# Branch projections of a hybrid encoder layer: operand loads in one written SyncE order, two k-pairs ahead, and the states' block sums formed inside the gate pairs

## The chip, the cores and the metric

The kernel runs on one core of one Trainium2 chip. The metric is the device time of one execution in microseconds (us); the median of several runs counts. TensorE is called PE here, VectorE DVE, ScalarE ACT, SyncE SP.

## The reference, cut to what matters

One encoder layer over 1024 tokens and 16 meta tokens, D_MODEL = 1024, all in float32. The part around the change is the middle of the layer:

```python
proj = h @ w_in                                  # split into q, k, v, z, ..., sc_b, sc_c, sc_x, gate_a, gate_b
o_dn = gated_deltanet_bidir(q, k, v, z, ...)     # its last step: o * silu(z)
y_a = o_dn @ w_branch_dn
y_b = (sc_b * depthwise_conv_centred(sc_c * sc_x, sc_conv_w)) @ w_branch_sc
merged = sigmoid(gate_a) * y_a + sigmoid(gate_b) * y_b
h_res = h_res + merged @ w_out
...
```

Before it lie the input projection with the DeltaNet scans, behind it the output projection, the SwiGLU and a final norm.

## The kernel before

**Arithmetic.** Every float32 operand is split into a high part (a cast on ACT, `split`, L101) and a low part (a subtraction on DVE, L102), and every product is three matmuls: high by high, high by low, low by high. The large products are done as 2 x 2 block products with seven block products instead of eight. Their operands are the blocks A11, A12, A22, B11, B21, B22 themselves and sums of blocks, S1 to S4 on one side and T1 to T4 on the other.

**Gate pairs.** The last thing that the input projection computes is the merge gates. A pair (`pair_steps`, L1574) takes two weight units of gates A and B, forms their block sums in place, does seven block products of 12 matmuls (named P1, P2, S2, S1, S3, S4, TT in the list `PAIR`, L1648) and puts the results into two tiles, o1 and o2, which are stored to `ta_d` and `tb_d` (L1622, L1623). Five pairs are done: pairs 0 and 1 in a hand-written order, pairs 2 and 3 by a loop (L1725), and the last one by `last_pair` (L1651). The result tiles come from the tag `s4` (L69), of which there are **four buffers**.

**States' sums.** `state_sums(k)` (L1700), four times, loads two rows of `p_d` (the short convolution's states) into two `s4` tiles, does four DVE subtractions of 512 columns and stores the result to `ts_d`. Before the change two of them are written behind each of pairs 2 and 3.

**Branch projections.** `blocks_of` (L1789) runs twice: first branch B (weights `w_bsc`, states from `p_d` and `ts_d`), then branch A (weights `w_bdn`, states `o_blocks`, which lie in SBUF). Each run goes over seven block products n = 0 to 6, each with two halves kk of the contraction. Here a half is called a k-pair and numbered q = 14*branch + 2*n + kk, so q = 0 to 27. A k-pair is 24 matmuls into four PSUM banks; products of even n go to one set of four banks, those of odd n to the other. Its operands are loaded by `loaded` (L1763, the DMA on L1767) into raw tiles, of which there are four buffers in rotation (branch B uses two a k-pair, branch A one), and split into a ring that holds the parts of four k-pairs.

After products 1, 4, 5 and 6 a quarter of the result is gated (`give`, L1801; DVE, L1805): for that, `gate_tiles` (L1793) has loaded four gate pieces into two `s4` tiles. In branch A the gated piece is also added to the other branch's (L1465).

`gated(h)` (L1715), eight times, loads a head's scan output into a big tile and its z into an `s4` tile, and multiplies them (L1723). When all eight are there, the A branch's own block sums (in `between_b(3)`) are formed on DVE: four subtractions of 128x2048 elements. `between_a` loads the eight rows of `w_out` into `s4` tiles (L1866) and splits them into the big tiles b0 to b3: four rows after product 5 of branch A, four after product 6.

Behind the projections come `merged` and `project` (L1887, L1895), whose matmuls are on L1899 to L1901.

**Order.** All these loads and stores are given out by SP. An SP instruction that waits for a buffer holds up all that stands behind it on SP. Where no manual schedule is open, the framework orders each engine's instructions by a simulation of its own, with the written order as priority; inside a manual schedule, the named engines keep the written order. Before the change nothing from pair 2 to the end of `blocks_of` is under a manual schedule.

Of the kernel before, what the change touches and what calls it, by code (L numbers as in the profile page):

```python
# [8 lines left out]
F32 = mybir.dt.float32  # L9
# [3 lines left out]
ALU = mybir.AluOpType  # L13
# [35 lines left out]
def encoder_layer(ctx: ExitStack, tc: tile.TileContext, x, meta, norm1_w, w_in, w_ba,  # L49
# [56 lines left out]
    def rawtile(shape):  # L106
        raw_slots.append(raw_slots.pop(0))
        pool, tag = raw_slots[-1]
        return pool.tile(shape, F32, tag=tag, name=uid("raw"), bufs=1)
# [1587 lines left out]
    for k in SECTION.split():  # L1697
        steps[k]()
    border0.close()
    def state_sums(k):  # L1700

        r = [s4(D) for _ in range(2)]
        for i in range(2):
            nc.sync.dma_start(r[i], p_d[4 * i + k])
        (b12, b11), (b22, b21) = ((t[:, lo], t[:, hi]) for t in r)
        sub(b11, b12, b11)
        sub(b12, b22, b12)
        sub(b22, b22, b11)
        sub(b21, b21, b22)
        for i in range(2):  # L1710
            nc.sync.dma_start(ts_d[k][:, i], r[i])
# [12 lines left out]

    for n, j in enumerate(range(GH + 2, KT - 1), 2):  # L1725
        d = pair_steps(n, j)[0]
        for k in PAIR.split():
            d[k]()
        for k in range(2):
            state_sums(2 * n - 4 + k)  # L1730
    o1 = last_pair(KT - 1 - GH, KT - 1)

    warm2 = keep.tile([P, 1], F32, name="warm2")
# [26 lines left out]
        split(h_, l_, src)  # L1760
        return h_, l_

    def loaded(f, kk):  # L1763

        raw = rawtile([P, 2, 512])
        for i in range(2):
            nc.sync.dma_start(raw[:, i], f(2 * kk + i))  # L1767
        return part(raw)

    def weight_blocks(w, sums_):  # L1770
        a = {"A11": (0, lo), "A12": (4, lo), "A22": (4, hi)}
        d = {n: lambda kk, r=r, c=c: loaded(lambda k: w[(r + k) * P:(r + k + 1) * P, c], kk) for n, (r, c) in a.items()}
        for n, i, c in (("S2", 0, lo), ("S3", 0, hi), ("S4", 1, lo), ("S1", 1, hi)):
            d[n] = lambda kk, i=i, c=c: loaded(lambda k: sums_[k][:, i, c], kk)
        return d

    state_blocks = {n: lambda kk, r=r, c=c: loaded(lambda k: p_d[r + k][:, c], kk)
                    for n, (r, c) in {"B11": (0, hi), "B21": (4, hi), "B22": (4, lo)}.items()}
    for n, i, c in (("T3", 0, lo), ("T1", 0, hi), ("T2", 1, lo), ("T4", 1, hi)):
        state_blocks[n] = lambda kk, i=i, c=c: loaded(lambda k: ts_d[k][:, i, c], kk)  # L1780

    bank_x, bank_y = [pss(), pss(), psd(), psm()], [psd(), psm(), pss(), psd()]
    pv, us = [], []

# [1 line left out]
        w = big("w2", [P, 2, 512], F32)  # L1786
        pv.extend([w[:, 0], w[:, 1], *(tp.tile([P, 512], F32, tag="t2", name=uid("t2"), bufs=2) for _ in range(2))])

    def blocks_of(a_, b_, gate_d, first, between):  # L1789

        gates = {}

        def gate_tiles(n, r, c):  # L1793
            g = [s4().rearrange("p (k c) -> p k c", k=2) for _ in range(2)]
            gates[n] = [g[t // 2][:, t % 2] for t in range(4)]
            for t in range(4):
                nc.sync.dma_start(gates[n][t], gate_d[r + t][:, c])

        where = {1: (0, hi), 4: (4, lo), 5: (0, lo), 6: (4, hi)}

        def give(n, t, y):  # L1801
            r, c = where[n]
            m_ = mg[r // 4][:, t, c]
            g = gates[n][t]
            nc.vector.scalar_tensor_tensor(out=m_ if first else g, in0=g, scalar=1.0, in1=y, op0=ALU.add, op1=ALU.mult)  # L1805
            if not first:
                add(m_, m_, g)
        for n, (a, b) in enumerate((("A11", "B11"), ("A12", "B21"), ("S2", "T2"), ("S1", "T1"), ("S3", "T3"), ("S4", "B22"), ("A22", "T4"))):
            bank = (bank_x, bank_y)[n % 2]
            fresh = n in (0, 1, 3)  # L1810
            if n in where:
                gate_tiles(n, *where[n])
            for kk in range(2):
                (ah, al), (bh, bl) = a_[a](kk), b_[b](kk)
                for t in range(4):
                    c = slice(t * P, t * P + P)
                    for k in range(2):
                        begin, end = kk + k == 0, kk + k == 2
                        mm(bank[t], ah[:, k, c], bh[:, k], start=begin and fresh, stop=False, skip_group_check=not fresh)
                        mm(bank[t], ah[:, k, c], bl[:, k], start=False, stop=False, skip_group_check=not fresh)  # L1820
                        mm(bank[t], al[:, k, c], bh[:, k], start=False, stop=end, skip_group_check=not fresh)
            if n == 0 and not pv:
                take_temps()
            if n == 2 and not us:
                w = [wp.tile([P, 2, 512], F32, tag=g, name=uid("us"), bufs=2) for g in ("wh", "wl")]
                us.extend(w[t // 2][:, t % 2] for t in range(4))
            for t in range(4):
                y = bank[t]
                if n in (0, 3):
                    nc.scalar.copy(pv[t], y)  # L1830
                elif n == 2:
                    nc.scalar.copy(us[t], y)
                elif n in (1, 4):
                    add(pv[t], y, pv[t])
                elif n == 5:
                    add(us[t], y, us[t])
            for t in range(4):
                if n in where:
                    give(n, t, (us if n == 5 else bank if n == 6 else pv)[t])
            between(n)  # L1840

    o_blocks = {}

    def between_b(n):
        if n < 2:
            for h in range(2):
                gated(4 + 2 * n + h)
        elif n == 3:
            t23 = big("b1", [P, 2, 4, 512], F32)
            t4 = big("b0", [P, 4, 512], F32)  # L1850
            b12, b11, b22, b21 = (og[i][:, :, c] for i in range(2) for c in (lo, hi))
            sub(t23[:, 1], b22, b12)
            sub(b12, b12, b11)
            sub(t23[:, 0], b22, b12)
            sub(t4, b21, t23[:, 0])
            for name, x in (("B11", b11), ("B21", b21), ("B22", b22), ("T1", b12), ("T2", t23[:, 0]), ("T3", t23[:, 1]), ("T4", t4)):
                o_blocks[name] = lambda kk, x=x: part(x[:, 2 * kk:2 * kk + 2])

    def between_a(n):
        nonlocal woh, wol  # L1860
        if n == 5:
            woh, wol = four("w")
        if n >= 5:
            for j in range(4 * (n - 5), 4 * (n - 5) + 4):
                raw = s4(D)
                nc.sync.dma_start(raw, w_out[j * P:j * P + P, :])  # L1866
                split(woh[j], wol[j], raw)

    woh = wol = None
    for h in range(4):  # L1870
        gated(h)
    blocks_of(weight_blocks(w_bsc, ss_d), state_blocks, tb_d, True, between_b)
    blocks_of(weight_blocks(w_bdn, sd_d), o_blocks, ta_d, False, between_a)

    wrow = big("w2", [P, D], F32)
    nc.sync.dma_start(wrow, norm2_w[0:1, :].broadcast_to([P, D]))
# [443 lines left out]
```

## Time and profile before

| | us |
|---|---|
| median of 3 runs | 1972.05 |
| the three runs | 1972.13, 1969.25, 1972.05 |
| the profiled execution | 1970.95 |
| its span (first to last instruction) | 1969.2 |
| PE busy in the span | 1939.6 (98%) |
| DVE busy | 1478.0 (75%) |
| ACT busy | 876.6 (45%) |
| mean granted PE clock (1 is full) | 0.995 |

Times in all rows are microseconds from the span's start. A row of a timeline has the start, the duration, the engine, the line, the operation, the tile written and the tiles read, how many instructions were merged into the row, and in brackets how long the engine sat idle before it and who ended that. SPq is SP's sequencer: its rows are the moments at which DMAs are given out, not their transfers. In a table of stretches each engine's cell is its busy time and its count of instructions; then come the granted PE clock, the mean busy share of the 16 DMA engines and the GB/s that they moved.

### The profile page before, as it was taken

The numbers are of one execution on the slowest core, as the hardware profiler recorded it, in microseconds if no ns is written. First come the engines' busy times: TensorE is split into PE (matmuls) and PEld (weight loads), VectorE is DVE, ScalarE is ACT, GpSimd is POOL, SyncE is SP. The second block draws the span as 40 slices with busy tenths as digits, with TensorE's granted clock in tenths as the row PEclk, the third lists the DMA queues.
The fourth block names the chain that finished last, engine by engine and source line by source line (L and its number), as shares of the span: only waits on it lengthen the run. The fifth ranks groups of instructions, "written<-read, shape, count | busy, mean of one in ns | idle before, by whom it ended". The sixth has DMA issues, their size and how long they took to land.

```text
span 1969.2 us, 32146 instructions
## 1 busy us (share of the span) xinstructions
PE 1939.6 (98%) x11896; PEld 1703.5 (87%) x11896; DVE 1478.0 (75%) x3117; ACT 876.6 (45%) x2016; POOL 109.4 (6%) x410
## 2 busy tenths in 40 slices
PE   9999999999999999999998899999999999999998
PEld 8999999999999999888886788888888888888887
DVE  7888688888888888867964777669676765746575
ACT  6472364646464646343443444335333333325344
POOL 2011101010101010100000000000000000000000
PEclk9999999999999999999999899999999999999999
DMA  4122122222221213375259863423366654577654
GB/s 145 59 89 79 57 87 60 76 60 76 60 78 58 85 51 108 108 260 206 86 205 346 288 197 120 147 102 115 110 230 245 246 189 153 179 277 239 194 175 166
DMA packets 141410, 286.15 MB, mean 145 GB/s; under 512 B 46844, under 2 KB 48309, under 8 KB 137797
## 3 DMA queue, kind: packets, MB, share of 16 engines
q1 hardware_dynamic: 140661, 283.05, 42.8%
q8 instruction: 93, 1.52, 0.3%
q10 hardware_dynamic: 592, 1.05, 0.1%
q14 instruction: 64, 0.52, 0.1%
HBM read 203.22 MB, written 80.83 MB: 144 GB/s over the span
## 4 chain that ended last, share of the span: by engine, by line
PE 88%; DVE 5%; DMA 5%; issue 1%; ACT 1%; SPq 0%; POOL 0%; DVEq 0%; ACTq 0%; POOLq 0%
PE pm L343 31%; PE pd L1499 12%; PE pe L1499 6%; PE pm L1499 4%; PE pd L907 1%; PE pd L886 1%; PE pd L871 1%; PE pd L868 1%; PE pe L605 1%; PE pe L2229 1%; PE pe L2228 1%; PE pe L2227 1%; PE pd L903 1%; PE pd L2229 1%; PE pd L2228 1%; PE pd L2227 1%
## 5 line engine op out<-in xcount | busy, mean ns | idle before, releaser
L343 PE MATMUL pm<-hTh,wh 128*128 128x320 f32 (+4 forms) x1248 | 426.6, 347 | 0.4 <-ACT hTh L1145 0.2
L343 PE MATMUL pm<-hTh,wl 128*128 128x320 f32 (+4 forms) x1248 | 426.5, 347 | 0.1
L343 PE MATMUL pm<-al,wh 128*128 128x320 f32 (+4 forms) x1248 | 424.4, 345 | 0.0
L343 PEld LDWEIGHTS pm<-hTh,wh 128*128 128x128 f32 x1248 | 233.8, 188 | 10.9 <-ACT hTh L1145 0.9
L343 PEld LDWEIGHTS pm<-al,wh 128*128 128x128 f32 x1248 | 233.8, 188 | 10.7
L343 PEld LDWEIGHTS pm<-hTh,wl 128*128 128x128 f32 x1248 | 233.9, 188 | 10.0 <-POOL wl L1160 0.3
L102 DVE TENSOR_TENSOR al<-raw,ring_h 128x1024 fp32r<-128x1024 f32 x73 | 88.8, 1223 | 65.4 <-ACT ring_h L101 64.9
L101 ACT CAST ring_h<-raw 128x1024 fp32r<-128x1024 f32 x73 | 76.7, 1053 | 107.5 <-PE pd L2229 37.4
L365 DVE SCALAR_TENSOR_TENSOR kq<-ra,wc,kq 128x520 f32<-128x520 f32 x128 | 96.6, 755 | 3.5 <-ACT kq L395 2.0
L998 DVE TENSOR_TENSOR wl<-raw,wh 128x512 fp32r<-128x512 f32 x112 | 75.2, 686 | 31.8 <-ACT wh L1001 31.6
L893 ACT ACTIVATE w<-pd,small 128x128 f32<-128x128 f32 x128 | 40.0, 363 | 128.2 <-PE pd L886 127.7
L498 DVE TENSOR_TENSOR tm<-fP,fN 128x135 f32<-128x135 f32 (+23 forms) x248 | 72.4, 292 | 4.9
L502 DVE TENSOR_TENSOR fP<-fP,tm 128x135 f32<-128x135 f32 (+23 forms) x248 | 71.9, 290 | 5.0
L1001 ACT CAST wh<-raw 128x512 fp32r<-128x512 f32 x112 | 66.0, 624 | 3.8 <-issue 3.6
L101 ACT CAST parts_h<-raw 128x1024 fp32r<-128x1024 f32 x36 | 37.8, 1054 | 66.7 <-PE pm L1820 26.3
L102 DVE TENSOR_TENSOR al<-raw,parts_h 128x1024 fp32r<-128x1024 f32 x36 | 43.4, 1223 | 29.9 <-ACT parts_h L101 29.7
L2167 ACT ACTIVATE b<-b 128x512 f32<-128x512 f32 x20 | 12.6, 632 | 104.6 <-DVE b L1465 104.6
L858 ACT ACTIVATE jk<-NP 128x128 f32<-128x128 f32 x64 | 19.9, 311 | 77.6 <-DVE NP L854 76.5
L1465 DVE TENSOR_TENSOR b<-pd,b 128x512 f32<-128x512 f32 x21 | 14.5, 690 | 51.1 <-PE pd L1499 51.1
L1499 PE MATMUL pd<-b_hl,wh 128*128 128x512 f32 x168 | 51.9, 390 | 0.0
L365 DVE SCALAR_TENSOR_TENSOR vT<-ra,wc,vT 128x520 f32<-128x520 f32 x64 | 48.4, 756 | 1.4 <-ACT vT L395 0.7
L694 POOL TENSOR_TENSOR tm<-mP,mN 1x15 f32<-1x15 f32 (+7 forms) x120 | 36.9, 308 | 211.6 <-DMA mN<-ndm 203.2
(699 smaller groups left out, 4855.6 us busy)
## 6 DMA issues: line engine op xcount, KB each, us to landing
raw<-in_w_in_dram SPq DMA_DIRECT2D x72, 512.0 KB
raw<-in_w_gate_up_dram SPq DMA_DIRECT2D x44, 512.0 KB
sums<-in_w_down_dram SPq DMA_DIRECT2D x22, 512.0 KB
t_d<-sums SPq DMA_DIRECT2D x11, 1024.0 KB
raw<-s_d SPq DMA_DIRECT2D x44, 256.0 KB
raw<-t_d SPq DMA_DIRECT2D x44, 256.0 KB
act_d<-b SPq DMA_DIRECT2D x43, 256.0 KB
raw<-act_d SPq DMA_DIRECT2D x33, 256.0 KB
```

The lines of the kernel that those rows point to most:

```text
L101: nc.scalar.copy(hi, src)
L102: nc.vector.tensor_tensor(out=lo, in0=src, in1=hi.bitcast(F32), op=ALU.subtract)
L343: mm(po[:, :n], ww[:, k], f(k)[:, t0:t0 + n], start=i == 0, stop=i == 3 * KT - 1)
L365: nc.vector.scalar_tensor_tensor(out=acc, in0=raw[:, h0 + t:h0 + t + hn], scalar=wc[:, t, col:col + 1], in1=acc, op0=ALU.mult, op1=ALU.add)
L498: nc.vector.tensor_tensor(out=tv, in0=fP[:, 0:r, j:j + 1].broadcast_to([P, r, n]), in1=fN[:, j:j + 1, j + 1:32].broadcast_to([P, r, n]), o ...
L502: nc.vector.tensor_tensor(out=fP[:, 0:r, j + 1:32], in0=fP[:, 0:r, j + 1:32], in1=tv, op=ALU.subtract)
L893: nc.scalar.activation(w[d], b2[:, 2 + d], AF.Copy, scale=ce[:, c, d:d + 1])
L998: nc.vector.tensor_tensor(out=u[1][1][:, k], in0=u[2][:, k], in1=u[1][0][:, k].bitcast(F32), op=ALU.subtract)
L1001: nc.scalar.copy(u[1][0][:, k], u[2][:, k])
L1499: mm(po, x[:, k], at(y, k), start=i == 0 and not add_to, stop=i == 11, skip_group_check=add_to)
L2227: mm(bank[t], h_[:, c], h_[:, hi], start=first, stop=False)
L2228: mm(bank[t], h_[:, c], l_[:, hi], start=False, stop=False)
```

## The change

The functions `loaded`, `weight_blocks`, `blocks_of`, `between_b` and `between_a` go, with the tables around them. In their place, `load(q)` gives out the DMAs of k-pair q's raw operands, and `products(q)` splits them, gives out `load(q + 2)`, does the 24 matmuls and then the additions and gates of the product. The table `beside` says what else is written behind each k-pair: the heads' gating, the gate pieces, the A branch's block sums and the rows of `w_out`. All 28 k-pairs stand inside a manual schedule for SP. `load(0)` is written ahead of the last gate pair. The arithmetic is the same; so are the tiles and their numbers of buffers. The loads of `state_sums` stand inside the pair, behind its steps P2 and sbl, and no longer behind the pair.

```diff
+    QUADS = (("A11", "B11"), ("A12", "B21"), ("S2", "T2"), ("S1", "T1"), ("S3", "T3"), ("S4", "B22"), ("A22", "T4"))
+    def load(q):
+        z, n, kk = q // 14, q % 14 // 2, q % 2
+        a, b = QUADS[n]
...
+        for x in (a, b)[:2 - z]:
+            raw = rawtile([P, 2, 512])
+            loads[q].append(raw)
+            for i in range(2):
...
+                nc.sync.dma_start(raw[:, i], src)
...
     for n, j in enumerate(range(GH + 2, KT - 1), 2):
         d = pair_steps(n, j)[0]
-        for k in PAIR.split():
+        for i, k in enumerate(PAIR.split()):
             d[k]()
-        for k in range(2):
-            state_sums(2 * n - 4 + k)
+            if i in (4, 16):
+                state_sums(2 * n - 4 + i // 16)
+    load(0)
     o1 = last_pair(KT - 1 - GH, KT - 1)
...
+    def gate_tiles(z, n):
+        r, c = where[n]
+        g = [s4().rearrange("p (k c) -> p k c", k=2) for _ in range(2)]
+        gates[z, n] = [g[t // 2][:, t % 2] for t in range(4)]
+        for t in range(4):
+            nc.sync.dma_start(gates[z, n][t], (tb_d, ta_d)[z][r + t][:, c])
+    where = {1: (0, hi), 4: (4, lo), 5: (0, lo), 6: (4, hi)}
+    def state_blocks():
+        t23 = big("b1", [P, 2, 4, 512], F32)
+        t4 = big("b0", [P, 4, 512], F32)
+        b12, b11, b22, b21 = (og[i][:, :, c] for i in range(2) for c in (lo, hi))
+        sub(t23[:, 1], b22, b12)
+        sub(b12, b12, b11)
+        sub(t23[:, 0], b22, b12)
+        sub(t4, b21, t23[:, 0])
...
+    def out_weights(js):
+        if not wo:
+            wo.extend(four("w"))
+        for j in js:
+            raw = s4(D)
+            nc.sync.dma_start(raw, w_out[j * P:j * P + P, :])
+            split(wo[0][j], wo[1][j], raw)
+    def products(q):
+        z, n, kk = q // 14, q % 14 // 2, q % 2
...
+        ah, al = part(loads[q][0])
+        bh, bl = part(loads[q][1] if z == 0 else o_blocks[QUADS[n][1]][:, 2 * kk:2 * kk + 2])
+        if q + 2 < 28:
+            load(q + 2)
...
+    beside = {0: [lambda: gated(0)], 1: [lambda: gated(1), lambda: gate_tiles(0, 1)], 2: [lambda: gated(2)],
+              3: [lambda: gated(3)], 4: [lambda: gated(4)], 6: [lambda: gated(5), lambda: gate_tiles(0, 4)],
+              8: [lambda: gated(6), lambda: gate_tiles(0, 5)], 9: [lambda: gated(7)], 10: [lambda: gate_tiles(0, 6)],
+              11: [state_blocks], 15: [lambda: gate_tiles(1, 1)], 20: [lambda: gate_tiles(1, 4)],
+              22: [lambda: gate_tiles(1, 5), lambda: out_weights((0, 1))], 23: [lambda: out_weights((2, 3))],
+              24: [lambda: gate_tiles(1, 6), lambda: out_weights((4, 5))], 25: [lambda: out_weights((6, 7))]}
+    stream = ExitStack()
+    stream.enter_context(tc.manual_schedule(engines={mybir.EngineType.SP}))
+    load(1)
+    for q in range(28):
+        products(q)
+        for f in beside.get(q, ()):
+            f()
+    woh, wol = wo
+    stream.close()
```

The gate pieces of product n in branch z, `gate_tiles(z, n)`, are used at the end of k-pair 14*z + 2*n + 1, as before.

More of the change, by code (lines that the diff above doesn't have):

```diff
@@ L1761, in part @@
         return h_, l_
[L1763 to L1780, printed above, removed]
     bank_x, bank_y = [pss(), pss(), psd(), psm()], [psd(), psm(), pss(), psd()]
@@ L1787, in take_temps @@
         pv.extend([w[:, 0], w[:, 1], *(tp.tile([P, 512], F32, tag="t2", name=uid("t2"), bufs=2) for _ in range(2))])
[L1789 to L1795, printed above, removed]
-            for t in range(4):
[L1797 to L1873, printed above, removed]
+    gates = {}
@@ new lines, in gate_tiles @@
+    def gate_tiles(z, n):
[5 more added lines that the diff above has]
+    where = {1: (0, hi), 4: (4, lo), 5: (0, lo), 6: (4, hi)}
+    o_blocks = {}
+    def state_blocks():
[6 more added lines that the diff above has]
+        sub(t4, b21, t23[:, 0])
+        o_blocks.update(B11=b11, B21=b21, B22=b22, T1=b12, T2=t23[:, 0], T3=t23[:, 1], T4=t4)
```

48 lines of the change are left out of this document (added).

## Prediction

> **What bounds the kernel now.** I read the page, then PE's waits, then the timelines of PE, SP, ACT and DVE around the branch projections, then a table of stretches.
>
> ```profile
> span 1969.2 us, 32146 instructions
> PE 1939.6 (98%) x11896; PEld 1703.5 (87%) x11896; DVE 1478.0 (75%) x3117; ACT 876.6 (45%) x2016; POOL 109.4 (6%) x410
> PE pe L1819 <- ACT wh L101: 10.2, 1, 10.2
> PE pd L1820 <- DVE al L102: 4.6, 1, 4.6
> ```
>
> PE bounds the kernel: an edit gains only where PE waits, and loses only where it makes PE wait. The two long waits are both in the branch projections.
>
> ```profile
> 1073.20 0.39 PE L1821 MATMUL pm<-b,wl 128*128 128x512 f32 x1
> 1083.82 0.80 PE L1819 MATMUL pe<-wh,b 128*128 128x512 f32 x1 [10.23 <-ACT wh L101]
> 1102.48 0.80 PE L1820 MATMUL pd<-al,parts_h 128*128 128x512 f32 x1 [4.55 <-DVE al L102]
> 1213.19 0.39 PE L1819 MATMUL pe<-parts_h 128*128 128x512 f32 x1
> 1234.95 0.39 PE L1899 MATMUL pe<-b,wh 128*128 128x512 f32 x1
> ...
> 1050.00:1073.40 23.40, 23.40 (x103) 18.76 (x101) 12.52 (x15) 7.41 (x12) 0.00 (x0) 1.00 0.97 358
> 1073.40:1110.00 36.60, 21.78 (x74) 16.76 (x74) 25.24 (x24) 10.98 (x11) 0.00 (x0) 0.77 0.90 328
> 1180.00:1235.00 55.00, 55.00 (x245) 45.53 (x244) 43.35 (x56) 24.73 (x30) 0.00 (x0) 1.00 0.41 135
> ```
>
> At 1073.20 the last matmul of k-pair 1 starts, at 1213.19 the first of 24, at 1234.95 the first of `project`. The last two are four k-pairs apart: 21.76 / 4 = **5.44 us a k-pair**. From 1073.43 the other 26 k-pairs would take 26 x 5.44 = 141.4 us; they take 161.5. So **20.1 us are lost**: 14.8 in the two waits, 5.3 (2.65 behind each) mostly in the slow matmuls that follow (granted clock 0.77 in that stretch; 1.00 around it). The stretch at the end, 1180 to 1235, runs without loss.
>
> Why the operands were late, on SP and ACT:
>
> ```profile
> 1060.64 1.76 SPq L1722 DMA_DIRECT2D s<-z_d  x2
> 1065.00 2.50 SPq L1722 DMA_DIRECT2D s<-z_d  x2
> 1069.36 0.40 SPq L1722 DMA_DIRECT2D s<-z_d  x1
> 1071.29 2.21 SPq L1797 DMA_DIRECT2D s<-tb_d  x4
> 1073.55 1.38 SPq L1767 DMA_DIRECT2D raw<-in_w_branch_sc_dram  x2
> 1075.86 1.61 SPq L1767 DMA_DIRECT2D raw<-p_d  x2
> 1081.31 1.04 ACT L101 CAST b<-raw 128x1024 fp32r<-128x1024 f32 x1 [7.09 <-DMA raw<-in_w_branch_sc_dram]
> ...
> s<-z_d SPq DMA_DIRECT2D x8, 512.0 KB
> raw<-p_d SPq DMA_DIRECT2D x8, 256.0 KB
> ```
>
> The loads of k-pair 2 leave SP at 1073.55, behind z tiles and gate pieces that wait for `s4` buffers one by one. The cast then waits for them until 1081.31.
>
> **The change, part by part.**
>
> *Front of branch B.* `load(1)`, `load(2)`, `load(3)` are now written ahead of most of the heads' gating, and `load(2)` needs only the raw buffers that the split of k-pair 0 frees, over 20 us before PE wants it. Ahead of it some 7 MB less must move (the scan and z tiles of six heads, four gate pieces). I take the whole 20.1 us as gained. Cover: PE has 10.9 us of k-pairs 0 and 1 around the last pair; if the loads come late all the same, up to 20.1 come back.
>
> *States' sums inside the pairs.* No instruction is added. But their two tiles now stand ahead of o2 of the same pair in the order of the four `s4` buffers.
>
> ```profile
> 1016.20 0.59 ACT L1615 COPY s<-pe 128x512 f32<-128x512 f32 x1 [2.17 <-PE pe L1499]
> 1012.62 0.85 SPq L1704 DMA_DIRECT2D s<-p_d  x2
> 1023.64 0.32 SPq L1711 DMA_DIRECT2D ts_d<-s  x1
> 1051.26 0.59 ACT L1659 COPY s<-pd 128x512 f32<-128x512 f32 x1 [1.41 <-DMA ts_d<-s]
> ```
>
> The first row is o2's first write in pair 2; rows two and three show that one state sum holds its buffers for 11 us and a store. The last row shows such a store already holding up a pair's copy. I estimate o2 to come some 4 us late in each of pairs 2 and 3, and S4, which adds to that bank, with it. The next pair's first products (12 matmuls, 2.72 us each by the k-pair's 24) can fill that. Between 0 and 2 x (4 + 2.65) = 13.3 I take **+1.0**, nearer to the fill.
>
> *End of branch B.* z of head 7 (behind k-pair 9) finds all four `s4` buffers held by the pieces of products 4 and 5, so it waits for the gating of k-pair 9; behind it on SP stand `load(12)`, the next pieces and `load(13)`.
>
> ```profile
> 1137.32 0.68 DVE L1465 TENSOR_TENSOR t<-pm,t 128x512 f32<-128x512 f32 x1
> 1137.92 0.68 DVE L1805 SCALAR_TENSOR_TENSOR mB<-s,w 128x512 f32<-128x512 f32 x1
> 1138.63 2.00 SPq L1797 DMA_DIRECT2D s<-tb_d  x4
> 1104.61 2.29 DVE L179 TENSOR_TENSOR b<-b 128x2048 f32<-128x2048 f32 x1
> 1215.89 1.29 DVE L1465 TENSOR_TENSOR mB<-mB,s 128x512 f32<-128x512 f32 x2
> 1118.83 0.80 SPq L1767 DMA_DIRECT2D raw<-ss_d  x2
> 1123.29 1.05 ACT L101 CAST parts_h<-raw 128x1024 fp32r<-128x1024 f32 x1 [2.03 <-DMA raw<-ss_d]
> ```
>
> By rows one to three a buffer comes free about 1.5 us after the end of k-pair 9 (E9; the addition of the last bank marks it), and by the last two a pair of loads takes 4.5 us to its cast. So `load(12)` is cast at about E9 + 8, in time for k-pair 12 at E9 + 10.9. But head 7's gating, done at about E9 + 6.4, sets free the A branch's four sums of 2.29 us, which are written ahead of k-pair 12's splits: DVE has these 9.2 us and product 5's eight additions and gates (0.6 each, by the pair of 1.29) before them. If all go first, the low parts end at E9 + 22.7: a stall of 11.6 + 2.65 = 14.3. If DVE slips the splits between them, 0. I take **+6.0**: the splits are ready in the middle.
>
> *End of branch A.* This is the largest term. Rows of `w_out` are written behind k-pairs 22, 23, 24 and 25, ahead of `load(25)`, `load(26)` and `load(27)`, and each needs an `s4` buffer while two products' gate pieces hold all four.
>
> ```profile
> 1189.17 5.38 SPq L1767 DMA_DIRECT2D raw<-in_w_branch_dn_dram  x4
> 1216.60 0.33 SPq L1866 DMA_DIRECT2D s<-in_w_out_dram  x1
> 1219.54 0.33 SPq L1866 DMA_DIRECT2D s<-in_w_out_dram  x1
> 1226.79 2.67 SPq L1866 DMA_DIRECT2D s<-in_w_out_dram  x2
> 1229.73 1.93 SPq L1797 DMA_DIRECT2D s<-ta_d  x4
> 1217.70 1.22 DVE L102 TENSOR_TENSOR al<-raw,parts_h 128x1024 fp32r<-128x1024 f32 x1
> 1218.83 0.68 DVE L1465 TENSOR_TENSOR mB<-mB,s 128x512 f32<-128x512 f32 x1
> 1220.83 1.05 ACT L101 CAST b<-s 128x1024 fp32r<-128x1024 f32 x1 [0.66 <-DMA s<-in_w_out_dram]
> ```
>
> Before, the last operands were given out from 1189.17, long ahead, and the weights waited alone: the first at 1216.60, as the pair of additions at 1215.89 freed one piece tile, the second at 1219.54, as the last addition freed the other: 3.4 and 6.3 us after k-pair 23 ends (E23 = 1213.19). Between the two DVE also did a split of 1.2 (1217.70), so 5.1 to 6.3. Now `load(25)` leaves behind the second weight. PE wants it at E23 + 5.44. With 0.33 for the issue, 4.5 us to the cast, up to 1.5 for the weight's 512 KB ahead of it (at 358 GB/s) and 1.05 for the cast, the high part is there at E23 + 11.0 to 13.7, a wait of 5.5 to 8.2: I take 7.0, in the middle, and 2.65 behind it: **+9.7**.
>
> `load(26)` needs two weights split; the first weight's cast was ready 4.2 us after its issue, so it lands while PE is late anyway: 0. `load(27)` stands behind two more gate tiles and two weights, so both tiles of product 5 must be free: by 1229.73, E25 + 5.7 (E25 = 1224.07). The same path gives a wait of 7.5; `project` for the first tokens needs none of product 6 and may fill up to four of it. I take **5.5 + 2.65 = 8.1**, between 3.5 and 10.2.
>
> In the Trainium skill, "TensorE: Matmul & The Clock Gate", Part 1, an idle window of about 3.4 us halves the clock, and about 3.4 us of work restores it: by that a gap costs 1.7 behind it, not the 2.65 that the trace gives. With it the two terms would be 1.9 lower in sum; the measured one is used.
>
> *Sum*, against the profiled execution (1970.95: its span 1969.2 and 1.75 around it; the median of the runs is 1.1 above it, and I correct nothing for that): -20.1 + 1.0 + 6.0 + 9.7 + 8.1 = +4.7, so **1975.7 us**. The front gap is moved to the back more than it is removed.
>
> **The rivals.**
>
> *Faster, the holds are short* (0.18). For it: PE's 5.44 us of k-pair 24 and `project` hide part; DVE may slip the splits. Bare waits of 7 at k-pair 25 and 3.5 at 27, no more: -20.1 + 10.5 = -9.6, **1961.4**. Against: the buffer count is four in all rows.
>
> *The weights hold nothing back* (0.12). If the written order let the operands past them, only the gain is left: **1950.9**. Against: under the manual schedule an instruction keeps its written place on SP, and 1219.54 shows that the buffer is waited for.
>
> *Slower: the pairs starve* (0.12). S4 of pairs 2 and 3 waits for o2 unfilled, from the point at which o2 comes later than one product (2.72 us) behind S3: 13.3 in place of 1.0, **1988.0**. For it: the row at 1051.26. Against: the other products are ready, splits and all.
>
> *The transfers bind* (0.08). From 1050 to 1073.4 the DMA engines were 0.97 busy at 358 GB/s, so the order might change nothing in when the bytes come. Half of the front loss stays: **1985.7**. In the Trainium skill, "DMA: Bandwidth & Descriptors", Specifications, the limit for a core is about 358 GB/s, which that stretch just meets. Against: only some 25 MB must land between 1050 and 1133, where k-pair 13 begins (twelve k-pairs, eight heads and four products' pieces, 1.05 MB each): 304 GB/s.
>
> **How the numbers follow.** The forecast has 0.50, and its own range is 1969 to 1982. The runs before spread over 0.15%, so 0.2% (3.9 us) is about what a measurement can tell from no change: 1968.1 to 1976.0. Faster: 0.18 + 0.12 = 0.30. Of the forecast's 0.50 some 0.28 lies below 1976.0: same. Slower: 0.22 + 0.12 + 0.08 = 0.42. The range 1957 to 1988.5 leaves out the full gain and the far ends.
>
> **What would show it.** Right: no wait at k-pair 2 or 4; new PE waits of 5 to 8 us on casts of the operands of k-pairs 25 and 27, with SP giving out `w_out` rows just before those loads; clock below 1 behind each; a wait on DVE's low part at k-pair 12 behind the 128x2048 subtractions. Wrong: PE unbroken from k-pair 22 to `project`, or operands given out while the `w_out` rows still wait; a wait at k-pair 2; PE idle inside pairs 2 and 3 (then the pairs starve).

## The result, and the profile after

The changed kernel takes **1983.9 us** (median of 4 runs, 1981.12 to 1985.54) against 1972.09 before (1969.25 to 1972.66): a ratio of **1.0061, 95% interval 1.0044 to 1.0079**. It is slower by 0.6%. The forecast was 1975.7, range 1957.0 to 1988.5, with 0.42 on slower. The profiled execution took 1981.12, with 1979.4 of span: 10.2 more than the profiled execution before. One experiment below (the sums put back) has no usable profile, since its profiled execution was disturbed; only its other times are used.

The page of the changed kernel, the busy time of its engines:

```profile
PE 1942.4 (98%) x11896; PEld 1704.8 (86%) x11896; DVE 1478.3 (75%) x3117; ACT 877.6 (44%) x2016; POOL 108.2 (5%) x410
```

The page alone shows nothing: every engine is as busy as before, to 3 us. The table of stretches of the changed kernel shows where PE stands:

```profile
1073.40:1110.00 36.60, 36.60 (x164) 30.29 (x163) 23.62 (x24) 18.38 (x23) 0.00 (x0) 1.00 0.99 357
1110.00:1150.00 40.00, 27.14 (x103) 21.16 (x102) 33.39 (x34) 11.08 (x11) 0.00 (x0) 0.83 0.59 205
1215.00:1240.00 25.00, 15.49 (x50) 11.17 (x49) 19.26 (x24) 10.14 (x12) 0.00 (x0) 0.80 0.69 228
```

In the first row stood the front gap (74 matmuls in the same 36.6 us before); now PE is unbroken, with the DMA engines 0.99 busy. The second and third rows hold new losses: at 0.2267 us a matmul (5.44 / 24), 103 and 50 of them take 23.3 and 11.3 us, so some 17 and 14 us are lost there, both stretches at a granted clock near 0.8. The gain at the front is real, and more than all of it is given back.

PE's timeline of the changed kernel, the rows at which it waits and the last rows ahead of two of the gaps:

```profile
1122.43 0.39 PE L1842 MATMUL pe<-parts_h,al 128*128 128x512 f32 x1
1126.14 0.50 PE L1840 MATMUL pe<-parts_h 128*128 128x512 f32 x1 [3.32 <-ACT parts_h L101]
1127.78 0.79 PE L1841 MATMUL pe<-al,parts_h 128*128 128x512 f32 x1 [0.44 <-DVE al L102]
1144.13 0.80 PE L1841 MATMUL pd<-al,parts_h 128*128 128x512 f32 x1 [9.11 <-DVE al L102]
1215.71 0.39 PE L1842 MATMUL pe<-parts_h,al 128*128 128x512 f32 x1
1222.34 0.80 PE L1840 MATMUL pe<-parts_h 128*128 128x512 f32 x1 [6.24 <-ACT parts_h L101]
1231.71 0.39 PE L1841 MATMUL pm<-al,parts_h 128*128 128x512 f32 x1
1235.33 0.50 PE L1911 MATMUL pe<-b,wh 128*128 128x512 f32 x1 [3.23 <-ACT wh L101]
```

k-pair 2 starts at 1073.70 here, and 9 x 5.44 later, at 1122.66, k-pair 11 should: that is the first wait. The second falls in k-pair 12, after its matmuls that need no low part. From 1122.43 to 1215.71 lie 14 k-pairs, 76.2 us of work in 93.3: **17.1 lost at k-pairs 11 and 12**, 12.9 of it in the waits and 4.2 in the slow matmuls behind them. Then **k-pair 25** waits 6.2, and **k-pair 26** stops in its middle, at 1231.71, until PE goes on with `project`. Adding up every spacing above 0.2267 on this timeline, each with its slow matmuls, gives 5.9 at k-pair 11, 11.3 at k-pair 12, 8.8 at 25 and 5.8 at 26: 31.8. The kernel before loses 20.1 in the front gap and 1.0 at the first tokens of `project`. That is 10.7 more, 0.5 above the measured difference of 10.2. This sum is called the loss below.

What PE waits for is on SP and DVE. SP's timeline of the changed kernel:

```profile
1105.63 0.32 SPq L1746 DMA_DIRECT2D s<-z_d  x1
1106.35 11.06 SPq L1802 DMA_DIRECT2D s<-tb_d  x4
1117.51 0.85 SPq L1722 DMA_DIRECT2D raw<-ss_d  x2
...
1213.67 1.53 SPq L1824 DMA_DIRECT2D s<-in_w_out_dram  x2
1215.24 0.91 SPq L1722 DMA_DIRECT2D raw<-sd_d  x2
1219.63 2.92 SPq L1824 DMA_DIRECT2D s<-in_w_out_dram  x2
1222.60 0.90 SPq L1722 DMA_DIRECT2D raw<-in_w_branch_dn_dram  x2
...
1235.03 0.91 SPq L1722 DMA_DIRECT2D raw<-in_w_branch_dn_dram  x2
```

The pieces of product 5 (L1802) take 11.06 us to give out, because the second of their tiles waits for the `s4` buffer of head 6's z. `load(11)`, at 1117.51, stands behind them. At the end the same picture twice: two rows of `w_out`, then `load(25)` at 1215.24, which k-pair 25 wanted cast by 1215.94; two more, then `load(26)`; the last row is `load(27)`.

DVE's timeline of the changed kernel:

```profile
1114.70 0.69 DVE L1465 TENSOR_TENSOR w<-pd,w 128x512 f32<-128x512 f32 x1 [0.67 <-PE pd L1842]
1115.31 1.28 DVE L1747 SCALAR_TENSOR_TENSOR b<-b,cols,s 128x1024 f32<-128x1024 f32 x1
...
1130.92 2.28 DVE L179 TENSOR_TENSOR b<-b,b 128x2048 f32<-128x2048 f32 x1
...
1134.91 2.49 DVE L1865 SCALAR_TENSOR_TENSOR mA<-s,us 128x512 f32<-128x512 f32 x4
1137.32 2.29 DVE L179 TENSOR_TENSOR b<-b 128x2048 f32<-128x2048 f32 x1
1139.52 1.22 DVE L102 TENSOR_TENSOR al<-raw,parts_h 128x1024 fp32r<-128x1024 f32 x1
1140.65 2.29 DVE L179 TENSOR_TENSOR b<-b,b 128x2048 f32<-128x2048 f32 x1
1142.86 1.22 DVE L102 TENSOR_TENSOR al<-raw,parts_h 128x1024 fp32r<-128x1024 f32 x1
...
1232.13 2.49 DVE L1465 TENSOR_TENSOR mA<-mA,s 128x512 f32<-128x512 f32 x4
1234.54 1.22 DVE L102 TENSOR_TENSOR al<-raw,parts_h 128x1024 fp32r<-128x1024 f32 x1
```

Head 6's gating (1115.31), which frees that z buffer, stands on DVE behind product 4's additions, which wait for PE bank by bank. At k-pair 12 two subtractions of the A branch and product 5's additions and gates go ahead of the first low part, a third subtraction ahead of the second. The bytes were there: by ACT's timeline of the changed kernel (first row) k-pair 12's second cast ended at 1131.40, some 8 us before DVE began the first of its low parts. At k-pair 26 the low part (1234.54) stands behind product 5's additions, though its cast was done 6 us earlier (second row). The third row is what `project` waits for, the cast of `merged`, behind the same additions:

```profile
1130.35 1.05 ACT L101 CAST parts_h<-raw 128x1024 fp32r<-128x1024 f32 x1 [0.58 <-DMA raw<-ts_d]
1227.44 1.05 ACT L101 CAST parts_h<-raw 128x1024 fp32r<-128x1024 f32 x1 [0.77 <-DMA raw<-in_w_branch_dn_dram]
1234.66 1.14 ACT L101 CAST wh<-mA 128x512 fp32r<-128x512 f32 x2 [6.16 <-DVE mA L1465]
```

### The profile page after: what moved, and what is told of

Its sections match the earlier page's. It is cut to its first block, busy times and chain, and to the rows that moved or that the text cites. A ratio compares the mean times of both kernels' runs of the same rounds, so it can differ in the third digit from the quotient of the medians.

```text
span 1979.4 us, 32121 instructions
## 1 busy us (share of the span) xinstructions
PE 1942.4 (98%) x11896; PEld 1704.8 (86%) x11896; DVE 1478.3 (75%) x3117; ACT 877.6 (44%) x2016; POOL 108.2 (5%) x410
## 4 chain that ended last, share of the span: by engine, by line
PE 92%; DVE 4%; DMA 2%; ACT 1%; issue 1%; SPq 0%; POOL 0%; ACTq 0%; DVEq 0%; POOLq 0%
PE pm L343 31%; PE pd L1499 14%; PE pe L1499 7%; PE pm L1499 5%; PE pd L907 1%; PE pd L886 1%; PE pd L871 1%; PE pd L868 1%; PE pe L605 1%; PE pe L2239 1%; PE pe L2240 1%; PE pe L2241 1%; PE pd L903 1%; PE pd L2239 1%; PE pd L2240 1%; PE pd L2241 1%
## 5 line engine op out<-in xcount | busy, mean ns | idle before, releaser
L343 PEld LDWEIGHTS pm<-al,wh 128*128 128x128 f32 x1248 | 233.8, 188 | 10.7
L998 DVE TENSOR_TENSOR wl<-raw,wh 128x512 fp32r<-128x512 f32 x112 | 75.4, 688 | 31.8 <-ACT wh L1001 31.5
```

The costliest lines, as they stand in the source:

```text
L343: mm(po[:, :n], ww[:, k], f(k)[:, t0:t0 + n], start=i == 0, stop=i == 3 * KT - 1)
L998: nc.vector.tensor_tensor(out=u[1][1][:, k], in0=u[2][:, k], in1=u[1][0][:, k].bitcast(F32), op=ALU.subtract)
```

## The experiments

**Theory.** In the written order, loads that wait for nothing of their own stand on SP behind transfers that wait for an `s4` buffer (k-pairs 11, 25, 26), and DVE has work ahead of splits (k-pairs 12, 26). **Rivals:** the bytes come late whatever the order; the written order or the short lead costs in itself; the waits are the `w_out` rows' own; and for DVE, that the additions of the product, not the subtractions, are what delays the splits. Ratios are to the kernel before.

### Branch A's loads four k-pairs ahead

```diff
-        if q + 2 < 28:
-            load(q + 2)
+        for r in ((q + 2,) if q < 12 else (14, 15) if q == 12 else (16, 17) if q == 13 else (q + 4,)):
+            if r < 28:
+                load(r)
```

> The changed kernel with one thing different: in the A branch (k-pairs 14 to 27) each load is written four k-pairs ahead instead of two, as far as the four raw buffers reach, so load(25), load(26) and load(27) stand on SP ahead of the w_out rows that wait for gate pieces. Theory 1 (SP's written order puts operands behind transfers that wait for a buffer): the losses at the end of branch A in the changed kernel, 8.7 us at k-pair 25 (6.4 idle and 2.3 in the slow matmuls behind it) and 5.9 at k-pair 26, go, some 0.9 of small waits of the kernel before stay at the first tokens; the losses at k-pairs 11 and 12 stay. 14 us less than the changed kernel: 1967 in a profiled run, 1970 as a median. Theory 2 (the waits at the end come from the w_out rows themselves, 4 MB at one time, or from ACT's and DVE's work on them, wherever the operands stand): k-pairs 25 and 26 wait as before, 1981 to 1984. Theory 3 (a written order on SP costs in itself, the buffers do not matter): little changes, 1978 to 1984.

Measured: 1974.96, ratio 1.0019 (1.0010 to 1.0029); profiled 1972.36. PE's timeline shows no wait at k-pair 25, and `project` still waits 2.92 at 1233.05. 8.8 us less in the profiled run, not 14: the loss at k-pair 25 is gone, so its cause was the load's late place on SP (this edit changes place and lead together; a later run keeps the lead of two). But `load(27)` still stands behind two `w_out` rows, and its low part behind product 5's additions on DVE. Some 1.6 of the rest is at k-pair 11, which the edit does not touch: it waits 4.99 here, against 3.32 and 0.44. So a difference of 1 to 2 us between two profiled runs should not be explained.

### Product 5's pieces behind load(11)

```diff
-              8: [lambda: gated(6), lambda: gate_tiles(0, 5)], 9: [lambda: gated(7)],
+              8: [lambda: gated(6)], 9: [lambda: gate_tiles(0, 5), lambda: gated(7)],
```

> The changed kernel with the four gate pieces of product 5 of branch B written one k-pair later, behind load(11) instead of ahead of it. Theory 1: load(11) no longer stands behind pieces that took 11.06 us to give out because they waited for the buffer of head 6's z; the loss at k-pair 11 (3.5 idle and 2.7 slow) goes. The loss at k-pair 12 (9.3 and 2.1) is DVE's order and stays, and may take a little more idle time since PE comes to it 6 us earlier while the subtractions do not come earlier: 0 to 6 us less than the changed kernel, 1975 to 1981 in a profiled run, nearer to 1978. If DVE reaches the subtractions by PE's clock (behind product 5's additions), the full 6. Theory 2 (the bytes come late whatever the order): load(11) is given out earlier and still lands at the same time, 1981.

Measured: 1976.57, ratio 1.0022 (1.0013 to 1.0032); profiled 1978.12. `load(11)` now leaves SP ahead of the pieces, 6 us earlier, and k-pair 11 does not wait (SP's timeline of this experiment):

```profile
1111.48 0.80 SPq L1722 DMA_DIRECT2D raw<-ss_d  x2
1113.88 5.65 SPq L1802 DMA_DIRECT2D s<-tb_d  x4
```

The wait at k-pair 12 stays (7.90). The cause at k-pair 11 is shown: the order on SP, not the bytes.

### The A branch's subtractions beside k-pairs 14 to 17

```diff
-        sub(t23[:, 1], b22, b12)
-        sub(b12, b12, b11)
-        sub(t23[:, 0], b22, b12)
-        sub(t4, b21, t23[:, 0])
+        blk.extend([(t23[:, 1], b22, b12), (b12, b12, b11), (t23[:, 0], b22, b12), (t4, b21, t23[:, 0])])
...
+              14: [lambda: sub(*blk[0])], 15: [lambda: sub(*blk[1]), ...], 16: [lambda: sub(*blk[2])], 17: [lambda: sub(*blk[3])],
```

> The changed kernel with the A branch's four subtractions of 128x2048 written one by one beside k-pairs 14 to 17 instead of all together beside k-pair 11. Theory 1: DVE then has k-pair 12's low parts right behind product 5's additions and gates, or before them; the loss at k-pair 12 (9.3 idle, 2.1 slow) goes down to 0 to 3 us: 8 to 11.4 less than the changed kernel, 1970 to 1973 in a profiled run. k-pairs 25 and 26 keep their losses. Rival (the low parts wait for product 5's eight additions and gates or for late operands, not for the subtractions): a wait of 5 us or more on the low part at k-pair 12 stays, 1976 or more. A second rival: the subtractions only move their cost to k-pair 18, the first that needs them: a new wait there.

Measured: 1980.27, ratio 1.0041 (1.0026 to 1.0056); profiled 1980.27. The first theory's 8 to 11 us did not come. DVE's timeline of this experiment, ahead of k-pair 12's matmul that waited until 1141.57 (5.15 us):

```profile
1132.76 2.28 DVE L179 TENSOR_TENSOR b<-b,b 128x2048 f32<-128x2048 f32 x1
...
1136.75 2.49 DVE L1864 SCALAR_TENSOR_TENSOR mA<-s,us 128x512 f32<-128x512 f32 x4
1139.16 4.63 DVE L102 TENSOR_TENSOR al<-raw,parts_h 128x1024 fp32r<-128x1024 f32 x4
```

Two of the three subtractions have gone; the first has not (DVE's order is the framework's own, so an instruction written later can be planned early), and product 5's additions and gates still stand ahead of the low parts. So the rival holds for part of this wait: 5.15 of 9.11 stayed, with one subtraction of 2.28 still ahead. k-pair 18 does not wait.

### The three together

> The three edits together: A branch's loads four k-pairs ahead, product 5's gate pieces behind load(11), the subtractions beside k-pairs 14 to 17. Theory 1: all four new losses go (6.2 + 11.4 + 8.7 + 5.9 = 32.2) and the 0.9 at the first tokens comes back: 1949 to 1951 in a profiled run, 1951 to 1954 as a median, some 20 us (1.0%) under the kernel before, which is the front gap alone. Rivals: if the transfers bind or the written order costs by itself, other k-pairs wait in place of these and it stays above 1965.

Measured: **1962.92, ratio 0.9958 (0.9943 to 0.9973)**: faster than both kernels, but some 10 above the expectation. Its loss is 13.8: 7.3 at k-pair 12, where PE waits 3.95 for a low part, and most of the rest at the end. DVE's and PE's timelines of this experiment:

```profile
1129.71 1.88 DVE L1865 SCALAR_TENSOR_TENSOR mA<-s,us 128x512 f32<-128x512 f32 x3
1131.52 2.35 DVE L102 TENSOR_TENSOR al<-raw,parts_h 128x1024 fp32r<-128x1024 f32 x2
1133.92 0.80 PE L1841 MATMUL pd<-al,parts_h 128*128 128x512 f32 x1 [3.95 <-DVE al L102]
```

No subtraction stands ahead of the low parts any more (the first is at 1133.79), and by ACT's timeline both casts were done by 1128.70. Product 5's additions and gates hold the low parts up: DVE's order is what is left, and not the transfers.

### The states' sums: put back, and alone

```diff
-        for i, k in enumerate(PAIR.split()):
+        for k in PAIR.split():
             d[k]()
-            if i in (4, 16):
-                state_sums(2 * n - 4 + i // 16)
+        for k in range(2):
+            state_sums(2 * n - 4 + k)
```

The first of two runs does this in the changed kernel, the second does the reverse alone in the kernel before.

> The changed kernel with the states' block sums put back behind each gate pair, as in the kernel before; everything else as changed. Theory 1 (the front gap went because of the order of the loads; the place of the sums is free): within 3 us of the changed kernel, 1978 to 1984 in a profiled run, no wait of over 1 us at k-pairs 2 to 4, the four losses as in the changed kernel. Rival (it was the sums' earlier place that let the first loads go): the wait at k-pair 2 comes back, 5 to 10 us more than the changed kernel, 1986 to 1992.

> The kernel before with one part of the change alone: the states' block sums inside the gate pairs. Theory 1: the z tiles and gate pieces still stand ahead of the loads on SP, so the front gap stays and the time is that of the kernel before within 4 us (1967 to 1975 in a profiled run). Rival: the sums' place removes a part of the front gap by itself, as the s buffers come free earlier: 1955 to 1966. Second rival (pairs starve): 1975 or more, with PE idle inside the last two pairs.

Measured: put back, ratio 1.0084 (1.0069 to 1.0100), its other three runs 1986.62 to 1990.78; alone, 1967.56, ratio **0.9980 (0.9971 to 0.9989)**. Alone they gain some 4 us. The time lies in theory 1's range, but the mechanism is the rival's: by SP's timeline of the second run the z tiles, at 1060.64 before, begin to go out at 1053.28. PE's timeline still has both front waits, the second of 4.55 as before, but the first is 6.47 and no longer 10.23.

```profile
1053.28 1.90 SPq L1722 DMA_DIRECT2D s<-z_d  x2
1080.28 0.80 PE L1819 MATMUL pe<-wh,b 128*128 128x512 f32 x1 [6.47 <-ACT wh L101]
```

Put back, the three runs have a median of 1986.80, 2.9 above the changed kernel's; by the two ratios it is 4.5, and their intervals overlap. Neither theory is decided, and without a profile it stays open where that time goes.

### SP's written order ended behind branch B

```diff
     for q in range(28):
+        if q == 14:
+            stream.close()
         products(q)
```

> The changed kernel with the written order on SP ended behind branch B: from k-pair 14 on SP's instructions are ordered as the framework plans them, with the same loads and the same lead in the program. Theory 1 (a fixed place on SP behind transfers that wait): the plan lets load(25) to load(27) past waiting w_out rows, and the losses at k-pairs 25 and 26 (14.6 us) shrink to 5 or less: 1968 to 1973 in a profiled run; k-pairs 11 and 12 as in the changed kernel. Rival (the buffers and the lead of two alone make them late; the written order is not the cause): k-pairs 25 and 26 lose what they lose in the changed kernel, 1978 to 1984.

Measured: 1978.74, ratio 1.0037 (1.0025 to 1.0049); profiled 1976.31. The losses at k-pairs 25 and 26 are gone: the plan lets the loads past the `w_out` rows (the last four transfers of branch A's weights go out from 1188.25). The lead in the program is still two, so the written order was the cause and not the lead. But the time is above the expected 1968 to 1973: a new wait of 5.75 us stands in the first tokens of `project`, on a low part of `merged` that DVE, by its timeline in this experiment, does behind product 6's additions, which those tokens do not need:

```profile
1240.42 0.69 DVE L1465 TENSOR_TENSOR mB<-mB,s 128x512 f32<-128x512 f32 x1
1241.02 1.29 DVE L102 TENSOR_TENSOR wl<-mA,wh 128x512 fp32r<-128x512 f32 x2
```

### More moved behind the loads

On top of the three edits: head 7's gating written beside k-pair 10, product 6's pieces beside 12, the `w_out` rows beside 23 to 26.

> The three edits of the fourth experiment and two more: head 7's z and the pieces of product 6 of branch B are written behind load(12) and load(14), and the w_out rows one k-pair later, so that load(27) stands ahead of them. The fourth experiment lost 6.9 us at k-pair 12, whose load stood behind head 7's z, and some 5 at the end, where load(27) stood behind two w_out rows and its low part behind product 5's additions. Theory 1: both shrink to 0 to 3 us each: 6 to 12 us less than the fourth experiment, 1951 to 1957 in a profiled run. Rival (DVE's order, product 5's additions and gates ahead of the splits, sets these two waits, wherever the loads stand): no gain, 1960 to 1965. Second rival: the w_out rows, later now, are what project waits for: a new wait of 3 to 8 us on the cast of a w_out row.

Measured: 1965.19, ratio 0.9969 (0.9956 to 0.9981). No gain: the low part at k-pair 12 waits 4.39, behind product 5's work as before, and at the end `project` waits 5.84 for a low part of `merged`, as in the run just told, and not for a `w_out` row. The first rival holds.

### Heads earlier, with a free and with a written end

```diff
-              3: [lambda: gated(3)], 4: [lambda: gated(4)], 6: [lambda: gated(5), lambda: gate_tiles(0, 4)],
-              8: [lambda: gated(6)], 9: [lambda: gate_tiles(0, 5), lambda: gated(7)], 10: [lambda: gate_tiles(0, 6)],
+              3: [lambda: gated(3)], 4: [lambda: gated(4)], 5: [lambda: gated(5)], 6: [lambda: gated(6)],
+              7: [lambda: gated(7), lambda: gate_tiles(0, 4)], 9: [lambda: gate_tiles(0, 5)],
+              12: [lambda: gate_tiles(0, 6)],
```

The first run besides closes the written order at k-pair 14 and writes branch A as the kernel before has it; the second keeps branch A of the fourth experiment.

> Branch B in the written order with three differences: heads 5, 6 and 7 are gated beside k-pairs 5, 6 and 7 (changed kernel: 6, 8, 9), the pieces of products 4, 5 and 6 stand behind load(9), load(11) and load(14), and the subtractions beside k-pairs 14 to 17. From k-pair 14 on everything as in the kernel before: SP's order left to the plan, each load and each product's pieces written at their use, the w_out rows behind products 5 and 6. Theory 1 (the losses came from loads behind transfers that wait, and from head gating and subtractions that DVE's planned order puts ahead of splits): k-pairs 11 and 12 lose 0 to 3 us together, the end of branch A under 1.5 as in the kernel before, the front nothing: 1951 to 1956 in a profiled run. Rival (DVE's order at k-pair 12 comes from product 5's additions and gates, not from the heads): 4 to 7 us lost at k-pair 12 as in the fourth and eighth experiments, 1956 to 1961. Second rival (transfers bind once three heads and their z, 1 MB each, move earlier): a new wait at k-pairs 4 to 9.

> Branch B as in the ninth experiment, branch A as in the fourth (written order to its end, loads four k-pairs ahead, w_out rows beside k-pairs 22 to 25). Theory 1: the same gain in branch B; the 5 us that the fourth experiment lost from k-pair 26 on stay, since there load(27) stands behind two w_out rows and its low part behind product 5's additions on DVE: 4 to 5 us more than the ninth, 1955 to 1961 in a profiled run. Rival (the written order at the end costs nothing once the loads stand early): the same time as the ninth within 2 us.

Measured: free end **1961.96, ratio 0.9953 (0.9940 to 0.9965)**; written end 1966.13, ratio 0.9972 (0.9962 to 0.9982). The end costs the difference, 4.2 us, as theory 1 has it: from k-pair 14 on the first has no wait but one of 0.3. In branch B the expected 0 to 3 us did not come: both lose 11 us, by the count of matmuls at k-pairs 10 and 12, on low parts again. PE's timeline with the free end:

```profile
1123.19 0.79 PE L1844 MATMUL pe<-al,parts_h 128*128 128x512 f32 x1 [4.55 <-DVE al L102]
1138.57 0.50 PE L1844 MATMUL pd<-al,parts_h 128*128 128x512 f32 x1 [2.82 <-DVE al L102]
```

### The next k-pair's splits ahead of the product's additions

The free-end kernel with one more edit in branch B: `operands(q)`, which does the splits of k-pair q, is called for the next k-pair ahead of the additions of this one. The second run also names DVE in the manual schedule (the last two lines).

```diff
+        if q < 13:
+            operands(q + 1)
         if not kk:
             return
...
-    stream.enter_context(tc.manual_schedule(engines={mybir.EngineType.SP}))
+    stream.enter_context(tc.manual_schedule(engines={mybir.EngineType.SP, mybir.EngineType.DVE}))
```

> The ninth experiment with one thing moved: in branch B the splits of k-pair q+1 are written ahead of the additions and gates of the product that ends with k-pair q; SP's order and the loads are unchanged, and DVE's order is still the plan's. The ninth lost 11 us at k-pairs 10 and 13, in waits for low parts (4.55 and 2.82) that DVE does behind additions that wait for PE. Theory 1 (what is left is DVE's order, not late bytes): the plan puts one of k-pair 10's two low parts ahead of product 4's gates and k-pair 12's ahead of product 5's additions: 3 to 8 us less than the ninth, 1953 to 1958 in a profiled run. Rival (the bytes are late): the same waits at the same places, 1959 to 1963.

> The eleventh experiment with DVE's order in branch B fixed as written, as SP's is: the low parts of k-pairs 10 to 13 stand ahead of the additions and gates of the product before. Theory 1: no low part waits behind an addition that waits for PE; the losses at k-pairs 10 and 13 go to 0 to 3 us in all, and the time is that of the front gap and the rest removed: 1950 to 1954 in a profiled run, some 1% under the kernel before. Rival (a low part now waits for bytes, and the additions behind it are late in turn): new waits of 3 us or more on ACT's casts or on the transfers at k-pairs 10 to 13, 1956 or more.

Measured: splits first **1955.3, ratio 0.9922 (0.9910 to 0.9934)**, 0.8% under the kernel before and the best version found; with DVE's order written too, 1961.75, ratio 0.9950 (0.9938 to 0.9963). In the first, one wait of 2.75 stays in branch B and the loss there is 5.8. PE's timeline and the table of stretches:

```profile
1120.73 0.80 PE L1852 MATMUL pe<-al,parts_h 128*128 128x512 f32 x1 [2.75 <-DVE al L102]
```

```profile
1073.40:1110.00 36.60, 36.60 (x163) 30.34 (x162) 24.99 (x25) 17.20 (x21) 0.00 (x0) 1.00 1.01 370
```

With the same loads, only the place of DVE's work was moved: the bytes were not late. With DVE's order written, the rival's 1956 or more came true: the splits stand behind heads' gating instead, which waits for z. DVE's timeline of the last run, whose PE waited 2.10 at 1107.38 for the last row:

```profile
1103.77 1.29 DVE L1747 SCALAR_TENSOR_TENSOR b<-b,cols,s 128x1024 f32<-128x1024 f32 x1 [4.65 <-DMA s<-z_d]
1104.97 2.36 DVE L102 TENSOR_TENSOR al<-raw,parts_h 128x1024 fp32r<-128x1024 f32 x2
```

So a fixed order moves the wait on DVE just as it did on SP.

## Why the prediction was right, and where it was not

**Front of branch B, -20.1: right.** The waits at k-pairs 2 and 4 are gone, and none stands elsewhere ahead of k-pair 11. How much of this the order of the loads does without the sums' earlier place is not shown, since the run with the sums put back has no profile.

**States' sums inside the pairs, +1.0: the hold right, a gain overlooked.** o2 does come late, by the forecast's path. ACT's timeline of the changed kernel has its first writes in pairs 2 and 3:

```profile
1019.48 0.59 ACT L1615 COPY s<-pe 128x512 f32<-128x512 f32 x1 [2.11 <-DMA ts_d<-s]
1041.46 0.58 ACT L1615 COPY s<-pe 128x512 f32<-128x512 f32 x1
```

Before they were at 1016.20 and 1035.27: 3.3 and 6.2 us late, where 4 was estimated. The other products filled it whole: PE has no wait in the pairs, and k-pair 2 starts at 1073.70 against 1073.43 at best before, 0.3 later at most. The working counted only what the sums' earlier place holds up. It left out what comes free earlier behind it: alone the sums gain 4 us at the front. In the changed kernel that gain can't be told from the front gap, which is gone in any case.

**k-pair 11, not in the sum: 5.9.** The working said that head 7's z finds all four buffers held, and that `load(12)` comes in time all the same. The hold came one step earlier, at product 5's pieces, with `load(11)` behind them. They waited for head 6's z, whose gating the prediction never followed on DVE. Moving the pieces took the wait away.

**k-pair 12, +6.0: mechanism right, size wrong, 11.3.** It was forecast between 0 and 14.3, with the middle taken; the wait fell near the upper end. Three subtractions and all of product 5's additions and gates went first. The subtractions are about half of it: in the fourth experiment none of them went ahead of the low parts, and 3.95 of the 9.11 stayed. The middle of a wide bracket was no estimate: the order on DVE decides, and nothing in the working said which order the framework would plan.

**k-pair 25, +9.7: right, 8.8** (forecast wait 7.0, measured 6.24).

**k-pair 26, forecast 0: wrong, 5.8.** Its load was forecast to land while PE is late anyway. It did, and was cast by 1228.5; but its low part waited on DVE for product 5's additions. The working followed the load to the cast on ACT and not to the split on DVE. That is the step that failed here.

**k-pair 27, +8.1: the path right, but hidden.** PE's timeline of the changed kernel shows 0.2 of wait:

```profile
1241.81 0.50 PE L1840 MATMUL pd<-parts_h 128*128 128x512 f32 x1 [0.21 <-ACT parts_h L101]
```

`load(27)` left SP at 1235.03, behind two more `w_out` rows as forecast, and was cast by 1241.76. k-pair 25 ends at 1230.13 here, so k-pair 27 would have wanted it at 1235.57: it was 6.2 us late. PE had lost nearly all of that time at k-pair 26 already, so only 0.2 shows. The two terms came near their sum (8.1 forecast, 5.8 measured) by luck.

**The price of a gap, 2.65 behind each: a little high.** The four gaps cost 2.1, 2.2, 2.5 and 2.4 behind their waits. In the Trainium skill, "TensorE: Matmul & The Clock Gate", Part 1, about 3.4 us of work at half clock restores the full one, by which, as an estimate, a gap costs 1.7. The measurement is between that and the price taken: the four together would be 6.8 by that estimate and measured 9.2.

In sum: +4.7 forecast, +10.2 measured between the profiled runs. k-pair 11 adds 5.9 and k-pair 12 5.3; the sums and the terms at the end came out 4.2 lower, and 1.0 that the kernel before lost at the first tokens of `project` is in the place where k-pair 26 now waits. That makes 6.0 more; 0.5 less was measured, and where that lies is open. The direction was right with its reason: the front gap moved to the back. That the number came within 8.2 us is in part luck, since a term that was left out (k-pair 11) and one too small by half (k-pair 12) were partly offset by terms that were too high.

The median lies just above the forecast's own 1969 to 1982, and nearer to the figure of "the transfers bind" (1985.7); the traces rule that rival out, and not the number: PE is unbroken at 0.99 DMA share. "The pairs starve" fell with the unbroken pairs, "the weights hold nothing back" with the wait at k-pair 25. "The holds are short" had the waits at the end nearly right (7 and 3.5; measured 6.2 and 3.2); it fell with the 17.1 us at k-pairs 11 and 12 and the slow matmuls behind each wait.

## What to carry to other kernels

When a load is given a fixed place on a queue, follow what stands ahead of it to its buffer, that buffer's last reader, and that reader's own place on its engine; the waits at k-pairs 11 and 25 were found on that path, and one edit took each away. Follow an operand to the last of its preparations, not the first: the splits on DVE, behind additions that wait for PE and behind subtractions, were more than half of the changed kernel's loss (k-pairs 12 and 26: 17 of 32) and nearly all of the best version's. Write the next tile's splits ahead of the additions that empty the last tile's banks, and fix an order by hand only as far as it earns its gain: written to the end of branch A it cost 4.2 us, and on DVE 6.5.

## What the runs showed of the hardware that was not expected

**How short a gap slows PE.** PE's timelines of three experiments, each from a wait on: the written DVE order, the heads earlier with a written end, and branch A's loads four k-pairs ahead.

```profile
1107.38 0.50 PE L1852 MATMUL pe<-al,parts_h 128*128 128x512 f32 x1 [2.10 <-DVE al L102]
1107.72 0.39 PE L1853 MATMUL pe<-parts_h,al 128*128 128x512 f32 x1
```

```profile
1224.95 0.79 PE L1913 MATMUL pe<-b,wh 128*128 128x512 f32 x1 [2.30 <-ACT wh L101]
1225.55 0.63 PE L1914 MATMUL pe<-b,wh 128*128 128x512 f32 x1
```

```profile
1233.05 0.50 PE L1912 MATMUL pe<-b,wh 128*128 128x512 f32 x1 [2.92 <-ACT wh L101]
1233.39 0.39 PE L1913 MATMUL pe<-b,wh 128*128 128x512 f32 x1
```

Behind 2.10 us of idle time the matmuls follow at 0.23 us. Behind 2.30, and behind the 2.75 of the best version, they follow at 0.43, for some 3 and 6 us. The Trainium skill, "TensorE: Matmul & The Clock Gate", Part 1, puts the idle window at about 3.4 us; here less was enough, though not each time: behind the 2.92 of the third fence they follow at 0.23 again. So no sharp threshold is shown between 2.1 and 3 us; all waits above 3.2 in these timelines were followed by slow matmuls. Where a short gap does slow PE, it costs about as much behind it as a long one (2.2 behind 9.11 of wait, 3.0 behind 2.75).

**Transfers beside an unbroken PE.** The best version moved 370 GB/s over 36.6 us (its row in the table of stretches), above the 358 that the Trainium skill, "DMA: Bandwidth & Descriptors", Specifications, gives as a core's limit and that the prediction took as a bound. The same page of the Trainium skill, section Bandwidth, says that a core alone can reach some 425, which that row does not contradict.
